# A decoder layer on one core: the down projection as seven block products

## The chip, the cores and the metric

The kernel runs on one core of a Trainium2 chip. The metric is the time of one execution on the device, in microseconds (us). TensorE does the matmuls, VectorE (DVE), ScalarE (ACT) and GpSimd (POOL) the rest, SyncE (SP) issues the transfers. Each engine takes its instructions in the order in which they were written for it. TensorE's order is written by hand; a scheduler lays out the others'.

## The reference

One layer for 1024 new tokens and 8 single ones (1032 columns in all), in fp32. This is the part around the change; `h` comes from two sequence mixers that share one input projection.

```python
h = rmsnorm(x, w['norm2_w'])
gate, val = jnp.split(h @ w['w_up'], 2, axis=-1)        # 1024 -> 2 x 2816
gate, buf_f_new = causal_dwconv(gate, buf_f, w['ffn_conv_w'], w['ffn_conv_b'])
x = x + (jax.nn.silu(gate) * val) @ w['w_down']         # 2816 -> 1024
...
y = rmsnorm(x, final_norm_w)
```

## The kernel before

The kernel is one stream of matmuls through four stages. Up to about 400 us run the input projections and the state-space mixer, from there to about 880 us the eight heads of the linear recurrence beside the rest of the input projections ("the heads"), then the output projection, from about 1056 to 1508 us the up projection, and from 1508 us the down projection with the final norm.

Data lies with features on partitions and tokens along the row. Every fp32 operand is split into a rounded part (ScalarE casts, `hi` or `wh`) and a remainder (VectorE subtracts, `lo` or `wl`), and each product is three matmuls: `wh*hi + wh*lo + wl*hi`. Weights come into `ws` (two buffers), tokens into `lo`, where they are split in place.

The up projection already uses seven products in place of eight block products (`ORDER`, class `Up`). It runs over 22 hidden tiles `j` of 128 features. For each, `up_load` fetches the weights of the next tile, GpSimd forms sums of them (`up_sums`), `up_split` splits them, 14 groups of 12 matmuls of 258 columns run (7 products x 2 token halves), and `up_close` does the convolution (ACT, then two taps on VectorE into `fcv`), SiLU, the product with `val`, and the store to `act_d`. The buffers of this stage (`fext`, `val`, `fcv`) come from one ring of five, `x5`.

The down projection contracts over the 22 hidden tiles in rounds of four (`RND`), five rounds, with the last two tiles apart. In a round each output tile `m` (8 of 128 features) meets four token quarters of 256, 256, 256 and 264; the partial sum in PSUM is added by VectorE to `xT[m]`, which holds the residual. The last two tiles run by token quarter, and after each quarter its token tiles are transposed by TensorE and go through the final norm (squares on ScalarE, root, scaling on VectorE, or ScalarE and GpSimd, store).

`tick()` stands after matmuls and runs work put there by `after(n, ...)`: it is written n ticks later. `spread(pieces, n)` writes one piece every n ticks. `fetch` puts a transfer behind the latest weight load on SP.

## Time and profile before

| | |
|---|---|
| median of 3 runs | 1781.38 us (1780.85 to 1782.73) |
| the profiled execution's own time | 1783.03 us |
| its span | 1781.3 us |
| mean granted TensorE clock | 0.994 |
| HBM read, written | 147.84 MB, 38.52 MB |

Rows of the profile read as follows. A group row gives line, engine, operation, out<-in, shapes, count, then busy time in us and mean ns of one, then the idle time just before on that engine and what ended it. A window row gives for each engine the busy us and the number of instructions, then the granted clock, the busy share of the transfer engines and GB/s. A wait row gives who waited for whom: us in total, times, longest. A timeline row gives start, duration, engine, line, and in brackets the idle time before. A tile row gives min, median and max ns, and the first and last start in us. `PE` is the matmul, `PEld` its weight load.

### The profile page before, as it was taken

Reading aid. Unit: us, or ns where it says so; the run is one execution under the profiler, and the core shown is the slowest. Engines: PE = TensorE matmul, PEld = TensorE weight load, DVE = VectorE, ACT = ScalarE, POOL = GpSimd, SP = SyncE. Lnnn points to the kernel's source line nnn. Section 1 sums busy time; section 2 is a strip of 40 time slices with the busy share of each in tenths; the row PEclk is TensorE's granted clock in tenths of the full one; section 3 lists DMA queues with packets and bytes.
Section 4 is the critical chain, followed back from the end, with each engine's and each line's share of the span. In section 5 each row is a group of like instructions: output and inputs, shape, how many; then the busy total and the mean of one; then the engine's idle time right before and its main releaser. Section 6 shows DMA issues by size and latency. Waiting matters only on the chain.

```text
span 1781.3 us, 38569 instructions
## 1 busy us (share of the span) xinstructions
PE 1740.1 (98%) x16223; PEld 1685.6 (95%) x16223; DVE 1118.6 (63%) x1949; ACT 797.7 (45%) x1413; POOL 394.5 (22%) x411
## 2 busy tenths in 40 slices
PE   7999999989999999999999999999999999999998
PEld 7999998989999999999999998999999999999997
DVE  4657888567655554556656678666666667545545
ACT  6477687444444444354344544334333344111114
POOL 1102142120110110111011234554445542000002
PEclk9999999999999999999999999999999999999999
DMA  5133575553222221224466432222222225422212
GB/s 155 36 88 84 150 209 151 141 168 106 66 78 63 76 82 43 82 79 127 145 193 200 125 114 72 72 72 78 81 92 72 72 82 204 152 82 90 97 60 96
DMA packets 240547, 188.66 MB, mean 106 GB/s; under 512 B 13356, under 2 KB 213590, under 8 KB 240358
## 3 DMA queue, kind: packets, MB, share of 16 engines
q1 hardware_dynamic: 240086, 186.11, 34.3%
q8 instruction: 127, 2.08, 0.5%
q14 instruction: 46, 0.38, 0.1%
q0 software_dynamic: 288, 0.10, 0.0%
HBM read 147.84 MB, written 38.52 MB: 105 GB/s over the span
## 4 chain that ended last, share of the span: by engine, by line
PE 72%; DVE 4%; DMA 2%; ACT 1%; issue 1%; DVEq 0%; POOL 0%; SPq 0%; ACTq 0%
PE mm L94 26%; PE ub L94 14%; PE dn L94 13%; PE ua L94 10%; PE a L94 3%; PE o L94 2%; PE kv L94 1%; DMA Sd<-in_state_ssm_dram 1%; DVE x L1260 1%; DMA ws<-in_w_out_dram 0%; PE ktp L960 0%; DVE wl L1056 0%; PE hms L94 0%; PE vtp L913 0%; DMA out_dram<-Sd 0%
## 5 line engine op out<-in xcount | busy, mean ns | idle before, releaser
L94 PE MATMUL mm<-hh,wh 128*128 128x344 f32 x1248 | 406.6, 326 | 0.0
L94 PE MATMUL mm<-hl,wh 128*128 128x344 f32 x1248 | 404.2, 324 | 0.0
L94 PE MATMUL mm<-hh,wl 128*128 128x344 f32 x1248 | 402.7, 323 | 0.0
L94 PEld LDWEIGHTS mm<-hh,wh 128*128 128x128 f32 x1248 | 234.9, 188 | 3.2 <-issue 1.1
L94 PEld LDWEIGHTS mm<-hl,wh 128*128 128x128 f32 x1248 | 234.9, 188 | 2.7 <-issue 1.1
L94 PEld LDWEIGHTS mm<-hh,wl 128*128 128x128 f32 x1248 | 235.0, 188 | 2.2 <-issue 1.0
L94 PE MATMUL ub<-uh,wh 128*128 128x258 f32 x704 | 199.5, 283 | 2.1 <-DVE fext L1431 1.6
L94 PE MATMUL ub<-ul,wh 128*128 128x258 f32 x704 | 199.9, 284 | 1.5 <-DVE ul L1292 1.5
L94 PE MATMUL ub<-uh,wl 128*128 128x258 f32 x704 | 199.0, 283 | 0.0
L94 PE MATMUL mm<-mx,wh 128*128 128x258 f32 x1024 | 191.3, 287 | 2.4 <-DVE mx L1072 2.0
L94 PE MATMUL dn<-ah,wh 128*128 128x256 f32 (+1 forms) x640 | 181.1, 283 | 1.0 <-DVE x L1556 0.9
L94 PE MATMUL dn<-ah,wl 128*128 128x256 f32 (+1 forms) x640 | 180.3, 282 | 0.0
L94 PE MATMUL dn<-al,wh 128*128 128x256 f32 (+1 forms) x640 | 180.3, 282 | 0.0
L189 ACT CAST wh<-ws 128x1024 fp32r<-128x1024 f32 x72 | 75.4, 1048 | 214.6 <-PE dn L94 136.0
L94 PEld LDWEIGHTS mm<-mx,wh 128*128 128x128 f32 x1024 | 159.2, 190 | 3.8 <-DVE mx L1072 2.4
L94 PE MATMUL ua<-uh,wh 128*128 128x258 f32 x528 | 150.1, 284 | 0.5 <-ACT us L1403 0.5
L94 PE MATMUL ua<-ul,wh 128*128 128x258 f32 x528 | 150.1, 284 | 0.0
L94 PE MATMUL ua<-uh,wl 128*128 128x258 f32 x528 | 149.9, 284 | 0.0
L94 PE MATMUL mm<-mx,wl 128*128 128x258 f32 x512 | 145.6, 284 | 1.5 <-DVE wl L1056 1.5
L94 PEld LDWEIGHTS ub<-uh,wh 128*128 128x128 f32 x704 | 133.0, 189 | 2.5 <-ACT uh L1270 1.8
L94 PEld LDWEIGHTS ub<-ul,wh 128*128 128x128 f32 x704 | 133.4, 189 | 1.9 <-DVE ul L1292 1.9
L94 PEld LDWEIGHTS ub<-uh,wl 128*128 128x128 f32 x704 | 133.4, 190 | 0.0
(339 smaller groups left out, 3747.6 us busy)
## 6 DMA issues: line engine op xcount, KB each, us to landing
ws<-in_w_in_dram SPq DMA_DIRECT2D x52, 512.0 KB
ws<-in_w_up_dram SPq DMA_DIRECT2D x44, 512.0 KB
ws<-in_w_out_dram SPq DMA_DIRECT2D x36, 512.0 KB
act_d<-val SPq DMA_DIRECT2D x22, 516.0 KB
al<-act_d SPq DMA_DIRECT2D x22, 516.0 KB
ws<-in_w_down_dram SPq DMA_DIRECT2D x22, 512.0 KB
mx<-mix_d SPq DMA_DIRECT2D x32, 258.0 KB
csb<-cs_d SPq DMA_DIRECT2D x32, 256.0 KB
```

What stands on the lines that cost most here:

```text
L94: PE.matmul(out, lhsT, rhs, start=start, stop=stop)
L189: A.copy(wh[:, :n], ws[:, :n])
L1260: V.scalar_tensor_tensor(x_, x_, col("n2", m), rs, op0=ALU.mult, op1=ALU.mult)
```

## The change

The down projection becomes seven block products over all 22 contraction tiles, one product after another. The 2816 features are paired, even tile with odd tile (11 pairs, `DK`); the 1024 outputs are cut into two halves of four tiles; the 1032 tokens into two halves of two spans (256 + 260 columns, `SPAN`). Each product takes a sum of token parts and a sum of weight parts (or a single part), and its result is added to or subtracted from several parts of `xT` (`PARTS`).

The token sums are formed in `up_close` (`act_sets`: two sums per even tile, six per odd) and stored to `act_d`, one plane per product. The weight sums are formed by GpSimd far earlier, while the heads run (`down_sums`, 22 pieces: two loads, four additions, one store to `wsum_d`), and are read back as weights of products p4 to p7.

A unit is one product for one output tile of the half: 66 matmuls (11 pairs x 3 x 2 token blocks). There are 28, the last product's being cut into single blocks at the end so that token tiles are finished in turn (`UNITS`). Weights are loaded two units ahead, split at tick 36 of the unit before; tokens are loaded and split during the product before. VectorE's splits are put behind the last eviction written (`pinned`). The final norm of a token tile runs after the unit that completes it (`FIN`); there is one more such tile, of four tokens. The ring `x5` becomes three rings, `xe`, `xc` and `xv` (six buffers). Half of the products' partial sums of the first five products now use four more PSUM tiles.

The diff, cut to its core:

```diff
-        "x5": (UW, 5), "us": (QW, 10), "t": (512, 4)}
+        "xe": (UW, 2), "xc": (UW, 1), "xv": (UW, 3), "us": (QW, 10), "t": (512, 4)}
...
+    wsum_d = dram.tile([2, 4, 2, P, DK, P], F32, name="wsum_d")
+    def down_sums():
+        src = w_down[0].rearrange("(i two p) (gv h c) -> h i p two gv c", two=2, p=P, gv=2, h=2)
+        for i in range(DK):
+            for h in range(2):
+                t = tl("g", "wq")[:, :DM]
+                for two in range(2):
+                    fetch(t[:, two * 512:(two + 1) * 512].rearrange("p (gv c) -> p gv c", gv=2), src[h, i][:, two])
+                yield
+                g1, v1, g2, v2 = (t[:, n * 256:(n + 1) * 256] for n in range(4))
+                for out, x_, y_ in ((v2, v1, v2), (v1, g1, v1), (g1, v2, g1), (g2, g1, g2)):
+                    G.tensor_tensor(out, x_, y_, op=ALU.add)
+                yield
+                SP.dma_start(wsum_d[h].rearrange("q m p k c -> p k (q m) c")[:, i],
+                             t.rearrange("p (q c) -> p q c", c=P))
+                yield
...
-    job("conv", None, once(lambda: spread(conv_states(), 60)))
+    job("conv", None, once(lambda: (spread(conv_states(), 60), spread(down_sums(), 26))))
...
-    act_d = dram.tile([FT, P, NT], F32, name="act_d")
+    act_d = dram.tile([7, DK, P, MID], F32, name="act_d")
+    PROD = ("p1", "p7", "p4", "p5", "p6", "p2", "p3")
+    SPAN = [[slice(0, 256), slice(256, 512)], [slice(512, 772), slice(772, NT)]]
+    BLOCK = [slice(0, 256), slice(256, MID)]
...
-        SP.dma_start(act_d[j], val[:, :NT])
+        spread(act_sets(j, ext, val), 6)
+    even = [None]
+    def act_store(name, i, t, c=None):
+        for n in range(2):
+            SP.dma_start(act_d[PROD.index(name), i, :, BLOCK[n]], t[:, BLOCK[n] if c is None else SPAN[n][c]])
+    def act_sets(j, ext, val):
+        i = j // 2
+        if j % 2 == 0:
+            even[0] = val
+            act_store("p1", i, val, 0)
+            yield
+            for n in range(2):
+                V.tensor_tensor(ext[:, BLOCK[n]], val[:, SPAN[n][0]], val[:, SPAN[n][1]], op=ALU.subtract)
+            act_store("p7", i, ext)
+            return
+        e = even[0]
+        act_store("p2", i, val, 0)
+        act_store("p4", i, val, 1)
+        yield
+        for n in range(2):
+            x_ = e[:, SPAN[n][1]]
+            V.tensor_tensor(x_, x_, val[:, SPAN[n][1]], op=ALU.subtract)
+        act_store("p5", i, e, 1)
+        yield
+        for n in range(2):
+            x_ = e[:, SPAN[n][0]]
+            V.tensor_tensor(x_, e[:, SPAN[n][1]], x_, op=ALU.subtract)
+        act_store("p6", i, e, 0)
+        yield
+        for n in range(2):
+            V.tensor_tensor(ext[:, BLOCK[n]], e[:, SPAN[n][0]], val[:, SPAN[n][0]], op=ALU.add)
+        act_store("p3", i, ext)
+    toks, wdn, evicted = {}, {}, [None]
+    def tok_open(n):
+        homes = ("hT",) * DK if n % 2 == 0 else ("hT",) * 5 + ("xe", "xe", "xc", "xv", "xv", "xv")
+        toks[n] = [tl(tag, "at", F32R) for tag in homes]
+    def tok_load(n, ks):
+        for k in ks:
+            SP.dma_start(toks[n][k][:, MID:NT].bitcast(F32), act_d[n, k])
+    def pinned(fn):
+        if evicted[0] is None:
+            return fn()
+        with tc.issue_after(evicted[0].ins):
+            fn()
+    def tok_split(n, ks):
+        for k in ks:
+            hi, lo = toks[n][k][:, :MID], toks[n][k][:, MID:NT]
+            A.copy(hi, lo.bitcast(F32))
+            pinned(lambda: V.tensor_tensor(lo, lo.bitcast(F32), hi.bitcast(F32), op=ALU.subtract))
+    SUMS = ("p6", "p5", "p4", "p7")
+    K1 = 8
+    def dw_load(u, n, m, pool):
+        name = PROD[n]
+        if name in SUMS:
+            src = wsum_d[m // 2, SUMS.index(name), m % 2]
+        else:
+            row, col_ = {"p1": (0, 0), "p2": (1, 0), "p3": (1, 512)}[name]
+            src = w_down[0].rearrange("(k two p) c -> two p k c", two=2, p=P)[row][:, :, col_ + m * P:col_ + (m + 1) * P]
+        ws = wpool.tile([P, KT * P], F32, tag="ws", bufs=2, name=nm("ws"))
+        w2 = pool.tile([P, KT * P], F32R, tag="wl", bufs=2, name=nm("w2"))[:, :(DK - K1) * P].bitcast(F32)
+        SP.dma_start(ws.rearrange("p (k m) -> p k m", m=P), src[:, :K1])
+        SP.dma_start(w2.rearrange("p (k m) -> p k m", m=P), src[:, K1:])
+        wdn[u] = pool, ws, w2
+    def dw_split(u):
+        pool, ws, w2 = wdn[u]
+        hi = pool.tile([P, KT * P], F32R, tag="wh", bufs=2, name=nm("wh"))
+        lo = pool.tile([P, KT * P], F32R, tag="wl", bufs=2, name=nm("wl"))
+        b = pool.tile([P, KT * P], F32R, tag="wh", bufs=2, name=nm("w2h"))
+        n = (DK - K1) * P
+        A.copy(hi, ws)
+        pinned(lambda: V.tensor_tensor(lo, ws, hi.bitcast(F32), op=ALU.subtract))
+        A.copy(b[:, :n], w2)
+        pinned(lambda: V.tensor_tensor(b[:, n:2 * n], w2, b[:, :n].bitcast(F32), op=ALU.subtract))
+        wdn[u] = [(hi, lo, k * P) if k < K1 else (b[:, :n], b[:, n:2 * n], (k - K1) * P) for k in range(DK)]
+    UNITS = [(n, m, (1, 0)) for n in range(6) for m in range(4)]
+    UNITS += [(6, 0, (1,)), (6, 1, (1,)), (6, 2, (1,)), (6, 3, (1, 0)), (6, 2, (0,)), (6, 1, (0,)), (6, 0, (0,))]
+    POOLS = [u % 2 for u in range(28)] + [None, 1, 0]
+    KEPT = {28: 26}
+    def unit_load(u):
+        if u < len(UNITS) and u not in KEPT:
+            dw_load(u, UNITS[u][0], UNITS[u][1], wpool if POOLS[u] else tmp)
+    def unit_split(u):
+        if u in KEPT:
+            wdn[u] = wdn[KEPT[u]]
+        elif u < len(UNITS):
+            dw_split(u)
+    def last_step(n):
+        if n == 3:
+            unit_load(0)
+            tok_open(0)
+        if n == 6:
+            tok_load(0, range(8))
+        if n == 9:
+            unit_split(0)
+            tok_load(0, range(8, 10))
+            tok_split(0, range(0, 4))
+        if n == 11:
+            tok_load(0, range(10, 11))
+            unit_load(1)
+            tok_split(0, range(4, 8))
+        if n == 12:
+            tok_split(0, range(8, 11))
...
+            if j == FT - 1:
+                last_step(n)
...
-        def down(w, kt, msl, acts, c):
-            q = quarters[c]
...
-                mm(ps, wh[:, msl], hi[:, q], start=(k == 0), stop=False)
-                mm(ps, wh[:, msl], lo[:, q], start=False, stop=False)
-                mm(ps, wl[:, msl], hi[:, q], start=False, stop=(k == kt - 1))
-            return ps
-        for r0 in range(0, FT - RND, RND):
...
-            for m in range(0, KT, 2):
-                wh, wl = wload(w_down[0, rows, m * P:(m + 2) * P], nk, 2 * P)
-                for i in range(2):
-                    for c, cs in enumerate(quarters):
-                        ps = down(lambda k: (wh[:, k, :], wl[:, k, :]), nk, slice(i * P, (i + 1) * P), acts, c)
-                        V.tensor_tensor(xT[m + i][:, cs], xT[m + i][:, cs], ps, op=ALU.add)
...
-    for c in (3, 0, 1, 2):
-        cs = quarters[c]
-        for m in range(KT):
-            ps = down(lambda k: wd[k], nk, slice(m * P, (m + 1) * P), acts, c)
-            V.tensor_tensor(xT[m][:, cs], xT[m][:, cs], ps, op=ALU.add)
-        for t0 in range(cs.start, cs.stop, P):
...
+        xT = [tl("big", "x1")[:, :NT] for _ in range(KT)]
+        for m in range(4):
+            for half_ in (0, 4):
+                SP.dma_start(xT[m + half_], x1_d[m + half_])
+        fw = tl("big", "fw")
+        SP.dma_start(fw[:, :DM], final_norm_w.unsqueeze(0).to_broadcast([P, DM]))
+        PARTS = {"p1": ((0, 0, 1), (0, 1, 1), (4, 1, 0), (4, 0, 0)), "p7": ((0, 1, 1), (4, 1, 0)), "p4": ((0, 1, 1),),
+                 "p5": ((4, 1, 1), (4, 0, 1)), "p6": ((0, 1, 1), (4, 1, 0), (4, 0, 0)), "p2": ((0, 0, 1),),
+                 "p3": ((4, 0, 1),)}
+        turn = [0]
+        def product(u, i):
+            n, m, _ = UNITS[u]
+            b = BLOCK[i]
+            turn[0] += 1
+            if n < 5 and turn[0] % 2:
+                ps = bank("dn")
+            else:
+                ps = psmm.tile([P, 512], F32, tag="mm", name=nm("dn"))
+            ps = ps[:, :b.stop - b.start]
+            for k in range(DK):
+                hi, lo = toks[n][k][:, b], toks[n][k][:, MID + b.start:MID + b.stop]
+                wh, wl, c0 = wdn[u][k]
+                wh, wl = wh[:, c0:c0 + P], wl[:, c0:c0 + P]
+                mm(ps, wh, hi, start=(k == 0), stop=False)
                 tick()
+                mm(ps, wh, lo, start=False, stop=False)
+                tick()
+                mm(ps, wl, hi, start=False, stop=(k == DK - 1))
+                tick()
+            for c0, c, plus in PARTS[PROD[n]]:
+                x_ = xT[m + c0][:, SPAN[i][c]]
+                evicted[0] = V.tensor_tensor(x_, x_, ps, op=ALU.add if plus else ALU.subtract)
+        def fin(t0, n, last):
...
-                if i and c != 2:
+                if i and not last:
...
+        FIN = {21: (256, P), 22: (384, P), 23: (772, P), 24: (900, 124), 25: (T, ND), 28: (512, P), 29: (640, P), 30: (768, 4)}
+        for u, (n, m, insts) in enumerate(UNITS):
+            after(2, lambda u=u: unit_load(u + 2))
+            after(36 if len(insts) > 1 else 6, lambda u=u: unit_split(u + 1))
+            if n < 6:
+                if m == 0:
+                    tok_open(n + 1)
+                if m < 3:
+                    ks = range(4 * m, min(4 * m + 4, DK))
+                    after(8, lambda n=n, ks=ks: tok_load(n + 1, ks))
+                if m:
+                    ks2 = range(4 * m - 4, min(4 * m, DK))
+                    pieces = (tok_split(n_, [k]) for n_ in [n + 1] for k in ks2)
+                    after(14, lambda pieces=pieces: spread(pieces, 12))
+            for i in insts:
+                product(u, i)
+            if u in FIN:
+                fin(*FIN[u], False)
+        for t0 in (0, P):
+            fin(t0, P, True)```

How it moves VectorE's order. First place: the end of the up projection and the first block of the down projection, before (`al`, `ah` are tokens, `wl` weight remainders, `x` the residual, `dn` the partial sum in PSUM):

```order
L1431 TENSOR_TENSOR fext_17732<-us_17843,ub_17892 128x258
L1431 TENSOR_TENSOR fext_17732<-us_17860,ub_17906 128x250
...
L190 TENSOR_TENSOR wl_18000<-ws_17998,wh_17999 128x1024
L1438 TENSOR_TENSOR val_17733<-us_17783,ua_17922 128x258
L356 SCALAR_TENSOR_TENSOR fcv_17950<-fext_17732,vcol,fcv_17950 128x1048
L1438 TENSOR_TENSOR val_17733<-us_17798,ua_17936 128x258
L356 SCALAR_TENSOR_TENSOR fcv_17950<-fext_17732,vcol,fcv_17950 128x1048
L1028 TENSOR_TENSOR al_17979<-al_17979,ah_17978 128x1032
L1556 TENSOR_TENSOR x_2353_18004<-x_2353_18004,dn_18006 128x256
L1454 TENSOR_TENSOR val_17733<-val_17733,fext_17732 128x1032
```

The same place on VectorE now (`at` are token tiles, L1501 to L1510 the sums of tokens, L1695 the evictions, `wl_18494` and `w2h_18495` the weights of unit 1):

```order
L1453 TENSOR_TENSOR fext_18110<-us_18240,ub_18314 128x258
L1533 TENSOR_TENSOR at_18195<-at_18195 128x516
L1533 TENSOR_TENSOR at_18196<-at_18196 128x516
L1453 TENSOR_TENSOR fext_18110<-us_18265,ub_18328 128x250
...
L1476 TENSOR_TENSOR val_18111<-val_18111,fext_18110 128x1032
L1695 TENSOR_TENSOR x_2374_18402<-x_2374_18402,dn_18431 128x260
L1501 TENSOR_TENSOR val_17842<-val_17842,val_18111 128x256
...
L1510 TENSOR_TENSOR fext_18110<-val_17842,val_18111 128x260
L1695 TENSOR_TENSOR x_2374_18402<-x_2374_18402,dn_18431 128x260
L1695 TENSOR_TENSOR x_2378_18406<-x_2378_18406,dn_18431 128x260 x2
L1558 TENSOR_TENSOR wl_18494<-ws_18345,wh_18493 128x1024
L1560 TENSOR_TENSOR w2h_18495<-w_2370_18346,w2h_18495 128x384
```

The splits of the last two token tiles of the first product now stand ahead of the last gate eviction, and the six sums and the block's evictions stand ahead of unit 1's weights.

Second place: SP in one of the heads, before (`ws` weights of the input projection, `Sh` a head's states, `vd` and `vb` its values on their way through memory):

```order
L179 DMA Sh_7196<-in_state_hgrn_dram 128x4x128
L179 DMA Sh_7200<-in_state_hgrn_dram 128x4x128
L977 DMA out_dram<-SS_7009 128x128
L186 DMA ws_7426<-in_w_in_dram 128x8x128
L855 DMA vd_d<-vd_7192 8x128
```

and now:

```order
L179 DMA wq_7469<-in_w_down_dram 128x2x256 x2
L179 DMA Sh_7288<-in_state_hgrn_dram 128x4x128
L179 DMA Sh_7292<-in_state_hgrn_dram 128x4x128
L1166 DMA wsum_d<-wq_7469 128x8x128
L977 DMA out_dram<-SS_7090 128x128
L186 DMA ws_7526<-in_w_in_dram 128x8x128
L179 DMA wq_7716<-in_w_down_dram 128x2x256 x2
L1166 DMA wsum_d<-wq_7716 128x8x128
L855 DMA vd_d<-vd_7284 8x128
```

Loads of down weights and the stores of their sums stand between the head's own transfers; each store waits for GpSimd's four additions.

41 lines of the change are left out of this document (6 added, 35 removed).

## The prediction

> **What bounds the kernel now.** I read the page's first part, then the table of windows over the last stages, then the waits of TensorE and the tiles of the stage that the change rewrites.
>
> ```profile
> span 1781.3 us, 38569 instructions
> PE 1740.1 (98%) x16223; PEld 1685.6 (95%) x16223; DVE 1118.6 (63%) x1949; ACT 797.7 (45%) x1413; POOL 394.5 (22%) x411
> ```
> ```profile
> core 0: us, PE busy (x) PEld busy (x) DVE busy (x) ACT busy (x) POOL busy (x), PEclk, DMA share, GB/s
> 300.00:400.00 100.00, 94.03 (x610) 90.19 (x609) 58.76 (x99) 45.16 (x98) 18.40 (x15) 0.97 0.58 166
> 700.00:800.00 100.00, 100.00 (x1430) 95.31 (x1428) 57.75 (x98) 44.58 (x67) 16.52 (x12) 1.00 0.25 74
> 1400.00:1500.00 100.00, 100.00 (x835) 100.00 (x834) 65.14 (x108) 38.79 (x69) 42.22 (x47) 1.00 0.31 99
> ...
> 1508.40:1741.20 232.80, 231.84 (x1943) 230.98 (x1943) 117.80 (x209) 41.67 (x42) 0.00 (x0) 1.00 0.29 98
> 1741.20:1771.70 30.50, 30.01 (x253) 29.15 (x252) 19.49 (x53) 16.66 (x43) 8.94 (x7) 1.00 0.26 96
> ```
>
> TensorE is busy for 98% of the span, and a busy bar alone proves little where matmuls overlap, so I take the spacing. In 1400 to 1500, 835 matmuls, nearly all 258 columns wide, take 100 us: 0.1198 us each. The down projection's five rounds hold 1943 in 232.80 us, again 0.1198. Two different stages with one spacing, the weight loads beside it as full, and a granted clock of 1.00: the stage is paced by the number of matmuls, not by what feeds them. The waits say the same.
>
> ```profile
> PE ub L94 <- DVE fext L1431: 1.6, 1, 1.6
> ...
> PE dn L94 <- DVE x L1556: 0.9, 1, 0.9
> ```
>
> In the down projection TensorE waited once, 0.9 us. VectorE, at 117.80 of 232.80 us, has half the stage free.
>
> **What goes.** The down projection has 22 contraction tiles x 8 output tiles x 4 token quarters x 3 products of halves = 2112 matmuls, of 256, 256, 256 and 264 columns, 258 on average. The block form has 7 products x 11 contraction tiles x 4 output tiles x 2 token blocks x 3 = 1848, of 256 and 260, again 258. So 264 x 0.1198 = **31.6 us** go from TensorE, if all that feeds it stays hidden.
>
> **What is added beside it.** The durations:
>
> ```profile
> L1556 DVE TENSOR_TENSOR x<-x,dn 128x256 f32<-128x256 f32 x120 | 49.8, 418 | 67.9 <-PE dn L94 67.9
> L190 DVE TENSOR_TENSOR wl<-ws,wh 128x1024 fp32r<-128x1024 f32 x20 | 24.5, 1223 | 8.1 <-ACT wh L189 8.0
> L189 ACT CAST wh<-ws 128x1024 fp32r<-128x1024 f32 x19 | 20.0, 1050 | 136.0 <-PE dn L94 136.0
> L1593 DVE SCALAR_TENSOR_TENSOR ot<-fin,fss,fw 128x512 f32<-128x512 f32 x10 | 7.3, 748 | 0.4
> ...
> L1381 DVE TENSOR_TENSOR wl<-ws,wh 128x512 fp32r<-128x512 f32 x63 | 43.4, 689 | 0.8
> L1522 DVE COPY cfr<-l 10x512 f32<-10x512 f32 x5 | 3.4, 677 | 0.1
> ```
>
> From 512 to 1024 elements VectorE's subtraction grows by 0.534 us, so I take 0.69 for 516, 0.55 for 384 and 0.41 for 256.
>
> The up projection (22 hidden tiles of 168 matmuls, 20.1 us each) gains 8 subtractions or additions per pair of tiles, 8 x 0.41 = 3.3 us in 40 us where VectorE has 35% free. They stand between two evictions of PSUM tiles that TensorE wants back four groups later. Price: nothing. SP's stores there rise from 2 to 14 per pair. They wait for these sums, and the next weight load waits behind them, but its first half is split only about 4 us after it lands, and is used in the next tile.
>
> The down stage: TensorE would need 1848 x 0.1198 = 221 us. VectorE has 112 evictions x 0.42 = 47, 77 token splits x 0.69 = 53, 30 weight splits x (1.22 + 0.55) = 53, and 20 us for the copies and the final norm: 173 us. It fits on average. In the first product it doesn't: 32 evictions (13.4), 4 weight splits (7.1), 11 token splits (7.6), the last hidden tile's convolution, product and six sums (7.1) and the first copy are 36 us in 31.6. So VectorE's order there has to be walked.
>
> **The entry into the first product.** Before, at the same place:
>
> ```profile
> 1507.25 1.26 ACT L354 ACTIVATE fcv<-fext,vcol 128x1048 f32<-128x1048 f32 x1 [0.54 <-DVE last L1435]
> 1511.54 1.06 ACT L1452 ACTIVATE fext<-fcv 128x1024 f32<-128x1024 f32 x1 [1.13 <-DVE fcv L356]
> ...
> 1508.60 1.30 DVE L356 SCALAR_TENSOR_TENSOR fcv<-fext,vcol,fcv 128x1048 f32<-128x1048 f32 x1
> 1512.85 1.22 DVE L1454 TENSOR_TENSOR val<-val,fext 128x1032 f32<-128x1032 f32 x1
> ```
> ```profile
> 1489.79 0.34 SPq L1511 DMA_DIRECT2D al<-act_d  x1
> ...
> 1493.32 1.06 ACT L1027 CAST ah<-al 128x1032 fp32r<-128x1032 f32 x1 [1.10 <-DMA al<-act_d]
> ```
>
> Let E be the end of the up projection (1508.4 before). TensorE starts the first block at once: its tokens come from even hidden tiles. But token tile 10 takes a buffer that TensorE frees at E-2.9 (two groups of twelve matmuls before E). Half the bytes of the load above (3.5 us from issue to use) I put at 2.5 to 3 us, so its cast ends near E+0.6 and its split at E+1.2. In VectorE's order that split stands ahead of the last gate eviction, which was ready at E-2.9. Then: evictions to E+2.2; ScalarE's start of the convolution, behind the weight cast of unit 1 (its load is issued at E-2.3), E+2.1 to 3.3; VectorE's two taps and an eviction to E+6.3; SiLU to 7.6; product to 8.8; one eviction, six sums, three evictions to 12.9; then unit 1's weight split, E+14.1. TensorE needs it at E+7.9 (66 matmuls): **6.2 us** lost. Were the loads early, the same walk gives E+9.7, 1.8 us. By the same steps units 2 and 3 arrive in time, and unit 4's split, behind four more token splits and a copy, is 1.7 us late. I take 7.9 us; bounds 2 and 12 (the latter if loads take 2 us more and both later units are also late). From the second product on a unit needs at most 7 of its 7.9 us on VectorE, and the debt is paid back.
>
> The short units at the end (4.0 us each) need 1.5 us of ScalarE and 1.8 of VectorE for weights and, by the tail's rows below, 2.6 and 1.1 for a tile of the final norm: together 4.1 and 2.9, just enough. Nothing; bound +5.
>
> **Transfers.** The stage moves 30 weight sets x 0.72 MB (128 x 1408 x 4 bytes), 77 token tiles x 0.264 and some 11 MB of residual, outputs and last stores, 53 MB in 221 us, 240 GB/s. The row 300 to 400 moved 166 GB/s at 0.58 busy, so 286 at full. They are issued a unit or more ahead. Nothing; the bound is a rival.
>
> **The heads.** 22 loads of down weights, 88 GpSimd additions and 22 stores run beside the head stage.
>
> ```profile
> L1416 POOL TENSOR_TENSOR val<-us,us x41: 735/757/1734, 1100.7 to 1502.9; 128x258 f32<-128x258 f32 x41
> L886 DVE TENSOR_TENSOR k<-k,tt x43: 680/693/1683, 421.9 to 860.0; 128x512 f32<-128x512 f32 x43
> ...
> DVE k L886 <- PE a L94: 57.3, 40, 2.8
> PE a L94 <- DVE q L887: 1.0, 1, 1.0
> ...
> 597.98 1.28 POOL L869 TENSOR_TENSOR Sh<-Sh,vb 128x512 f32<-128x512 f32 x1
> L94 PE MATMUL od<-Sh,qb x16: 272/273/297, 621.0 to 621.4; 128*32 128x128 f32 x16
> ```
>
> 88 x 0.75 = 66 us of GpSimd, which is 17% busy there. Each store holds SP until load and sums are done, about 6 us (a load of some 3 us, as above, and four sums of 0.75). What is queued behind it, the small transfer of v to memory and the head's state update, ends at 599.3 before and is used at 621.0: 22 us of cover. VectorE waits 1.4 us per level (57.3 / 40) for TensorE, so delays below that vanish. I take 0.6 us; bounds 0 and 35 (below).
>
> **The tail.** From the last matmul to the span's end there are 9.6 us. Now a four-token tile stands ahead of the last two tiles of the final norm.
>
> ```profile
> L1583 ACT ACTIVATE ot<-fin 128x512 f32<-128x512 f32 x16 | 9.4, 595 | 30.2 <-PE fin L1581 28.6 <-PE dn L94 0.9 <-DMA out_dram<-ot 0.3
> L1590 ACT ACTIVATE ot<-fin,fss 128x512 f32<-128x512 f32 x6 | 4.1, 687 | 1.3 <-DVE fss L1586 1.3
> L1583 ACT ACTIVATION_READ_ACCUMULATOR ot<-fin 128x1 f32 x16 | 3.2, 198 | 0.0
> L1585 ACT ACTIVATE fss<-fss,epsc 128x1 f32<-128x1 f32 x8 | 2.4, 296 | 2.3 <-DVE fss L1584 2.3
> ...
> 1771.40 0.28 PE L94 MATMUL dn<-ah,wdl 128*128 128x256 f32 x1
> ...
> 1776.56 1.41 DVE L1593 SCALAR_TENSOR_TENSOR ot<-fin,fss,fw 128x512 f32<-128x512 f32 x2
> ```
>
> It puts 2 x 0.79 us of squares, a root and a scaling on ScalarE, and 0.75 on VectorE, ahead of them, and takes two of the four PSUM tiles. Walking the steps the last output is ready 8.4 us after the last matmul, where it was 6.3: **+2.1 us**, bounds 0.5 and 3.
>
> **Sum.** -31.6 + 7.9 + 0.6 + 2.1 = -21.0 us. The profiled run's span is 1781.3, its own time 1783.03 and the median 1781.38; a saving inside the span shifts all three, so 1781.38 - 21.0 = **1760.4 us**.
>
> **Rivals.** (1) All is hidden: 1781.4 - 31.6 + 2.1 and 2 at the entry = 1754. For it: half-idle VectorE; against: the walk above. 0.22.
>
> (2) VectorE and ScalarE stay late. If each of the first three products lost what the first does, the stage would lose 7.9 x 3: 1776. For it: every weight split stands behind an eviction of the same unit, so debt moves on to TensorE; against: the later units' surplus. 0.10.
>
> (3) Slower: GpSimd's sums block the heads. L886 takes 0.69 us, and up to 1.68, one GpSimd instruction more. A run of four sums is 3 us; if all 22 runs met a level of the scan chain and each cost 3.0 - 1.4 us, 35 us, then 1760.4 + 35 = 1795. It turns the sign where a run costs over 0.95 us. Against it: TensorE waited once on this chain, 1.0 us, although GpSimd ran 3 us runs there already. 0.04. The Trainium skill (SBUF — State Buffer, Who interferes with whom) says that a VectorE instruction with two SBUF inputs and a GpSimd instruction that reads SBUF share a port pair held for a whole instruction. By that rule up to 66 us of VectorE's time would go, still within its free 40% of about 370 us, and the sum would stand; the 1.68 us row agrees with the rule.
>
> (4) Transfers bind. At 200 GB/s the 53 MB would take 265 us, 44 more than TensorE needs: 1760.4 + 44 = 1804. Against it: the 286 above. 0.02.
>
> **How the numbers follow.** The forecast has 0.62. Eight times in ten the time lies from 1751 (rival 1 with the tail hidden) to 1776 (rival 2). A measurement of this kernel can tell about 0.2%, 3.6 us. Faster than 1777.8: the forecast, rival 1 and most of rival 2, 0.92; within: 0.03; slower: rivals 3 and 4, 0.05.
>
> **What would show it.** Matmuls 264 fewer at an unchanged 0.12 us; between E and E+40 one or two waits of TensorE on VectorE's weight split, 6 and 2 us; none on DMA later; no new wait in the heads; the tail 11 to 12 us. It is wrong if the spacing in the later products grows, or if the heads take over 3 us more.

## The result, and the profile after

The changed kernel takes 1759.99 us (median of 4 runs, 1758.13 to 1761.37) against 1781.12 for the kernel before; the ratio is 0.9884, 95% interval 0.9872 to 0.9896. The forecast was 1760.4. The total came out right; the terms of the sum did not, and this section says where.

The first lines of the page and TensorE's waits behind the up projection, in the changed kernel (waits: who for whom, us in total, times, longest):

```profile
span 1756.2 us, 39052 instructions
...
PE 1710.0 (97%) x15967; PEld 1655.9 (94%) x15967; DVE 1173.3 (67%) x2053; ACT 844.8 (48%) x1512; POOL 482.8 (27%) x500
```
```profile
PE dn L94 <- DVE wl L1558: 3.9, 1, 3.9
PE fin L1702 <- DVE ot L1714: 1.8, 1, 1.8
```

256 matmuls fewer (264 in the down projection, 8 transposes of the final norm more), and two new waits: one on VectorE's split of weights, the one the forecast walked to, and one in the tail. This span is 25.1 us shorter than that of the first profile of before, while the medians differ by 21.1. One pair of profiles is too little for terms of a few us, so I cut every trace of this study into the same stages. A stage runs from the first start of one kind of matmul to the first or last start of another, as the tile rows give them: the heads from the first `a` to the last `o`, the output projection from there to the first `ua`, the up projection to the first `dn`, the down projection to the last `dn`, the tail to the end of the span. For the heads these are the two rows of the changed kernel, 883.6 - 401.4 = 482.2 us:

```profile
L94 PE MATMUL a<-q,k x3456: 176/196/270, 401.4 to 868.2; 128*32 128x32 f32 x160, 128*16 128x16 f32 x32
...
L94 PE MATMUL o<-q,SS x112: 275/275/275, 442.6 to 883.6; 128*128 128x128 f32 x112
```

| trace | to the heads | heads | output proj. | up | down | tail |
|---|---|---|---|---|---|---|
| before, first trace | 401.3 | 481.6 | 173.2 | 452.4 | 262.9 | 9.9 |
| before, second (rep_before) | 402.7 | 479.5 | 172.8 | 452.4 | 263.3 | 9.8 |
| changed, first | 401.4 | 482.2 | 173.6 | 452.4 | 233.9 | 12.7 |
| changed, second (rep_after) | 398.4 | 483.9 | 174.2 | 451.2 | 235.4 | 12.7 |
| fin4_early | 404.5 | 484.4 | 173.4 | 451.7 | 236.6 | 9.8 |
| split1_only | 402.5 | 487.4 | 175.3 | 452.4 | 235.6 | 12.7 |
| split1_load2 | 405.5 | 484.4 | 173.8 | 451.2 | 236.5 | 12.7 |
| entry_nofin | 402.4 | 485.4 | 173.0 | 451.2 | 234.2 | 12.7 |
| entry_split12 | 403.7 | 485.3 | 173.8 | 452.3 | 228.8 | 12.7 |
| best_safe | 400.5 | 486.4 | 173.6 | 451.7 | 230.4 | 9.8 |
| no_sum_adds | 401.9 | 478.3 | 174.2 | 451.1 | 235.1 | 13.2 |
| no_sum_all | 399.6 | 479.4 | 173.7 | 450.5 | 235.3 | 13.1 |
| sum_memset | 400.7 | 479.4 | 174.1 | 450.6 | 233.6 | 12.7 |
| sums_up | 402.5 | 479.8 | 173.3 | 537.4 | 235.1 | 12.7 |

Eight traces (from changed, first, to best_safe) have the heads, the output projection and the up projection unaltered. Their means against the two of before: to the heads +0.4, heads +4.4 (484.9 against 480.55), output projection +0.8, up -0.6; down -28.45 and tail +2.85 from the two traces of the changed kernel. The sum is -20.6, in agreement with the medians. The first trace of the changed kernel is that of the fastest of its four executions (1758.13 us) and has the shortest heads of the eight; the first trace of before is that of an execution at 1783.03, above the median. The two differ by 24.9 us, and that made the 25.

The wait at the entry, in the changed kernel. First VectorE's timeline (start, duration, engine, line; E, the end of the up projection, is 1509.6), then windows of 2 to 4 us with TensorE's matmuls and its granted clock (third column from the right):

```profile
1515.99 1.23 DVE L1476 TENSOR_TENSOR val<-val,fext 128x1032 f32<-128x1032 f32 x1 [1.29 <-ACT fext L1475]
1517.14 0.42 DVE L1695 TENSOR_TENSOR x<-x,dn 128x260 f32<-128x260 f32 x1
1517.48 0.76 DVE L1501 TENSOR_TENSOR val<-val,val 128x256 f32<-128x256 f32 x2
1518.15 0.76 DVE L1506 TENSOR_TENSOR val<-val 128x256 f32<-128x256 f32 x2
1518.83 0.76 DVE L1510 TENSOR_TENSOR fext<-val,val 128x256 f32<-128x256 f32 x2
1519.50 1.09 DVE L1695 TENSOR_TENSOR x<-x,dn 128x260 f32<-128x260 f32 x3
1520.51 1.22 DVE L1558 TENSOR_TENSOR wl<-ws,wh 128x1024 fp32r<-128x1024 f32 x1
```
```profile
1517.50:1521.50 4.00, 0.36 (x3) 0.15 (x2) 4.00 (x11) 0.00 (x0) 0.00 (x0) 1.00 0.68 179
1521.50:1523.50 2.00, 1.72 (x8) 1.73 (x9) 2.00 (x6) 0.00 (x0) 0.00 (x0) 0.59 1.06 374
1523.50:1525.50 2.00, 2.00 (x12) 2.00 (x12) 0.01 (x1) 0.00 (x0) 0.00 (x0) 0.56 0.88 231
1525.50:1527.50 2.00, 2.00 (x19) 2.00 (x19) 0.17 (x1) 0.26 (x1) 0.00 (x0) 1.00 1.10 333
```

Product, six sums and evictions, then unit 1's weights: the order of the forecast's walk. The split of `wl`, the remainder that TensorE waits for, ends at 1521.73, E+12.1 (E+13.0 in the second trace), where the walk said E+14.1. The windows show what the walk did not have: after the gap the granted clock is 0.56 to 0.59, and TensorE starts 12 matmuls in 2 us where it starts 19 afterwards. It stays so for about 3.6 us, some 16 matmuls at 0.216 us in place of 0.118: another 1.6 us.

The tail, TensorE's and ScalarE's timelines in the changed kernel:

```profile
1747.37 1.10 PE L1702 MATMUL fin<-ident,x 128*128 128x128 f32 x8 [1.80 <-DVE ot L1714]
...
1748.81 0.60 ACT L1704 ACTIVATE ot<-fin 128x512 f32<-128x512 f32 x1 [1.10 <-DMA out_dram<-ot]
...
1750.36 0.60 ACT L1704 ACTIVATE ot<-fin 128x512 f32<-128x512 f32 x1 [0.86 <-DMA out_dram<-ot]
```

The last token tile waits for a PSUM tile, as forecast, and then twice for the store of an earlier output, since the `ot` tiles come from a ring of four buffers and the extra tile of four tokens takes two of them.

### The profile page after: what moved, and what is told of

Its sections match the earlier page's. It is cut to its first block, busy times and chain, and to the rows that moved or that the text cites. A ratio compares the mean times of both kernels' runs of the same rounds, so it can differ in the third digit from the quotient of the medians.

```text
span 1756.2 us, 39052 instructions
## 1 busy us (share of the span) xinstructions
PE 1710.0 (97%) x15967; PEld 1655.9 (94%) x15967; DVE 1173.3 (67%) x2053; ACT 844.8 (48%) x1512; POOL 482.8 (27%) x500
## 4 chain that ended last, share of the span: by engine, by line
PE 70%; DVE 5%; issue 1%; ACT 1%; DMA 1%; POOLq 0%; DVEq 0%; POOL 0%; ACTq 0%
PE mm L94 25%; PE ub L94 14%; PE dn L94 12%; PE ua L94 11%; PE a L94 2%; PE o L94 2%; PE kv L94 1%; DVE k L886 1%; DVE x L1282 1%; DVE q L887 1%; DMA ws<-in_w_out_dram 1%; DVE wl L1056 1%; PE ktp L960 0%; PE hms L94 0%; PE vtp L913 0%
## 5 line engine op out<-in xcount | busy, mean ns | idle before, releaser
L94 PE MATMUL mm<-hh,wh 128*128 128x344 f32 x1248 | 407.1, 326 | 0.0
L94 PE MATMUL mm<-hl,wh 128*128 128x344 f32 x1248 | 404.6, 324 | 0.0
L94 PE MATMUL mm<-hh,wl 128*128 128x344 f32 x1248 | 403.2, 323 | 0.0
L94 PEld LDWEIGHTS mm<-hh,wh 128*128 128x128 f32 x1248 | 235.4, 189 | 3.2 <-issue 1.1
L94 PEld LDWEIGHTS mm<-hl,wh 128*128 128x128 f32 x1248 | 235.4, 189 | 2.7 <-issue 1.1
L94 PEld LDWEIGHTS mm<-hh,wl 128*128 128x128 f32 x1248 | 235.3, 189 | 2.2 <-issue 1.0
L94 PE MATMUL ub<-uh,wh 128*128 128x258 f32 x704 | 199.5, 283 | 2.1 <-DVE fext L1453 1.6
L94 PE MATMUL ub<-ul,wh 128*128 128x258 f32 x704 | 199.9, 284 | 1.5 <-DVE ul L1314 1.5
L94 PE MATMUL ub<-uh,wl 128*128 128x258 f32 x704 | 199.0, 283 | 0.0
L94 PE MATMUL mm<-mx,wh 128*128 128x258 f32 x1024 | 191.0, 286 | 1.6 <-DVE mx L1072 1.2
L94 PE MATMUL dn<-at,wh 128*128 128x260 f32 (+1 forms) x896 | 164.3, 284 | 0.0
L94 PEld LDWEIGHTS mm<-mx,wh 128*128 128x128 f32 x1024 | 158.5, 189 | 3.3 <-DVE mx L1072 1.7
L94 PE MATMUL ua<-uh,wh 128*128 128x258 f32 x528 | 150.2, 284 | 0.5 <-ACT us L1425 0.5
L94 PE MATMUL ua<-ul,wh 128*128 128x258 f32 x528 | 150.2, 284 | 0.0
L94 PE MATMUL ua<-uh,wl 128*128 128x258 f32 x528 | 149.9, 284 | 0.0
L94 PE MATMUL mm<-mx,wl 128*128 128x258 f32 x512 | 145.4, 284 | 1.7 <-DVE wl L1056 1.7
L94 PEld LDWEIGHTS dn<-at,wh 128*128 128x128 f32 x896 | 138.9, 190 | 0.0
L94 PEld LDWEIGHTS ub<-uh,wh 128*128 128x128 f32 x704 | 133.0, 189 | 2.5 <-ACT uh L1292 1.8
L94 PEld LDWEIGHTS ub<-ul,wh 128*128 128x128 f32 x704 | 133.4, 189 | 1.9 <-DVE ul L1314 1.9
L1164 POOL TENSOR_TENSOR wq<-wq 128x256 f32<-128x256 f32 x88 | 82.1, 933 | 189.6 <-DMA wq<-in_w_down_dram 184.4
L94 PEld LDWEIGHTS ub<-uh,wl 128*128 128x128 f32 x704 | 133.4, 190 | 0.0
L94 PE MATMUL dn<-at,wl 128*128 128x260 f32 (+1 forms) x448 | 127.4, 284 | 3.9 <-DVE wl L1558 3.9
```

What stands on the lines that cost most here:

```text
L94: PE.matmul(out, lhsT, rhs, start=start, stop=stop)
L1164: G.tensor_tensor(out, x_, y_, op=ALU.add)
```

## Experiments: the terms repeated

The changed kernel and the kernel before, unaltered, for second traces.

> The changed kernel once more, nothing altered. The first pair of profiles differs by 25 us in span, the medians by 21 us, and my sum of terms gave 21. Theory A: the terms are those of the first trace (entry wait 3.9 us plus 1.6 us at a lower clock, heads +0.7, tail +2.9), the trace was a fast one by chance, and the scatter of 3 us between executions lies ahead of the up projection: the second trace shows the same 3.9, 0.7 and 2.9 within 0.5 us, time 1758 to 1761. Theory B: the scatter lies in the entry, where the weights come through a busy transfer queue: the wait differs by over 1 us between the two traces.

Measured: 1759.93 us (0.9887, 0.9867 to 0.9907). The entry wait was 4.9 us instead of 3.9, the heads 483.9 instead of 482.2, the stretch ahead of them 398.4 instead of 401.4; the tail was the same. Neither theory holds alone: the entry scatters by 1 us, and the heads by 1.7 and the part ahead of them by 3.

> The kernel before once more, nothing altered, for a second trace: the heads (first a matmul to last o matmul) took 481.5 us in the first trace of before and 482.2, 483.9, 484.4, 487.4 and 484.4 in five traces of changed kernels. Theory A (the down weights' sums in the heads cost more than the forecast's 0.6 us, 2 to 5 us): before's second trace gives 481 to 482.5. Theory B (the heads scatter by themselves): it gives 483 or more.

Measured: 479.5 us of heads, below the 481 to 482.5 of theory A and further still from theory B's 483. Before is at or below its first trace, and all eight traces with the sums lie above both, which is theory A's point; but the two traces of before are 2.1 us apart, so the heads scatter too.

## Experiments: the sums in the heads

In no_sum_adds the four additions per piece are taken out, as below; in no_sum_all the whole `spread(down_sums(), 26)`, and the products p4 to p7 read parts of the down weights in place of their sums:

```diff
-                for out, x_, y_ in ((v2, v1, v2), (v1, g1, v1), (g1, v2, g1), (g2, g1, g2)):
-                    G.tensor_tensor(out, x_, y_, op=ALU.add)
```

> The changed kernel with GpSimd's 88 additions of down weights left out; the 44 loads and the 22 stores stay, so what is stored is the loaded parts and not their sums. Theory A (GpSimd's instructions hold VectorE and the head's state update): the heads go back to 481.5 to 482.5 us and the time falls by 2 to 3 us. Theory B (the transfers: SyncE's queue, and TensorE's instructions that come through the same transfer engines, its waits of 1.6 to 3.1 us with no releaser): the heads stay at 483 to 485 us, time within 1 us of 1760.

> The changed kernel with the loads, additions and stores of the heads all left out; products p4 to p7 read parts of the down weights in place of their sums, the same number of bytes. Both theories of no_sum_adds: the heads go back to 481.5 to 482.5 us and the waits of TensorE without a releaser vanish there; the time falls by 2 to 3 us, to 1757 to 1758. If the heads stay at 484 us, neither the additions nor the transfers are the cause.

Measured: 1755.12 us (0.9857, 0.9836 to 0.9878) and 1754.97 (0.9857, 0.9837 to 0.9877), heads 478.3 and 479.4. That is 5 us less than the changed kernel, twice the 2 to 3 us of theory A, and the same within the scatter with and without the 44 loads and 22 stores. So the additions cost it, and the transfers nothing that shows.

What is it about the additions? sum_memset keeps GpSimd busy as long, without reading:

```diff
-                for out, x_, y_ in ((v2, v1, v2), (v1, g1, v1), (g1, v2, g1), (g2, g1, g2)):
-                    G.tensor_tensor(out, x_, y_, op=ALU.add)
+                for c in (0, 256, 0, 256):
+                    G.memset(t[:, c:c + 768], 1.0)
```

> The 88 additions of down weights replaced by 88 GpSimd memsets of 768 columns, 0.73 us each by the traced 0.98 us for 1032: GpSimd is held as long, but reads nothing from SBUF; the stored parts are constants. In the changed kernel VectorE's busy time between 430 and 800 us is 219 to 224 us against 206 in before and in no_sum_adds, and L886's mean rises from 0.76 to 0.87 us. Theory A (VectorE and GpSimd share a port to SBUF, and each VectorE instruction that meets an addition takes longer): with memsets VectorE's busy time there returns to 206 to 209 us, the heads to 478 to 481 us, and the time is 1755 as in no_sum_adds. Theory B (GpSimd's own queue: the head's state update and the small transfers wait behind four instructions in a row): the heads stay at 483 to 485 us and the time at 1760.

Measured: 1755.47 us (0.9859, 0.9843 to 0.9876), heads 479.4. Below, for the second trace of before, the second of the changed kernel, and sum_memset, each time first the window 430 to 800 (PE, PEld, DVE, ACT and POOL busy us, clock, DMA share, GB/s), then groups within it: a step of the scan chain, and GpSimd's work on the down weights (count, busy us, mean ns).

```profile
430.00:800.00 370.00, 369.48 (x4811) 351.89 (x4810) 206.79 (x372) 160.15 (x246) 49.79 (x36) 1.00 0.25 73
```
```profile
L886 DVE TENSOR_TENSOR k<-k,tt 128x512 f32<-128x512 f32 x35 | 27.5, 786 | 46.1 <-PE a L94 46.1
```
```profile
430.00:800.00 370.00, 365.15 (x4760) 347.68 (x4759) 220.78 (x370) 158.99 (x243) 130.33 (x124) 1.00 0.45 132
```
```profile
L886 DVE TENSOR_TENSOR k<-k,tt 128x512 f32<-128x512 f32 x34 | 31.0, 912 | 44.7 <-PE a L94 44.7
...
L1164 POOL TENSOR_TENSOR wq<-wq 128x256 f32<-128x256 f32 x88 | 80.8, 918 | 191.2 <-DMA wq<-in_w_down_dram 154.7 <-DVE qb L856 31.3
```
```profile
430.00:800.00 370.00, 369.35 (x4827) 351.51 (x4826) 208.07 (x372) 160.50 (x247) 114.83 (x124) 1.00 0.45 133
```
```profile
L886 DVE TENSOR_TENSOR k<-k,tt 128x512 f32<-128x512 f32 x35 | 27.7, 791 | 46.4 <-PE a L94 46.4
...
L1164 POOL MEMSET wq<- 128x768 f32 x88 | 65.5, 745 | 201.7 <-DMA wq<-in_w_down_dram 167.3 <-DVE qb L856 30.6
```

GpSimd is busy for 65 us more than before in sum_memset, and VectorE only 1.3 us more; with additions VectorE has as many instructions as before (370 against 372), 14 us more to do, and the step of the chain takes 912 ns instead of 786. TensorE is busy 365.15 us of the window instead of 369.4. Its waits in this window, first in the second trace of before (sum_memset has the same one row), then in the second of the changed kernel:

```profile
PE cst L342 <- DVE od L671: 0.5, 1, 0.5
```
```profile
PE a L94 <- issue: 2.3, 2, 1.3
PE a L94 <- DVE q L887: 2.1, 4, 0.8
...
```

About half of the loss is TensorE waiting for a step of the chain (L887 is the step behind L886). The other half are waits for which the profile shows no releaser (`issue`). All eight traces with the additions in the heads have such waits before `a` matmuls, 1.3 to 3.1 us in the heads, and the other six have none: the additions bring them, but in what way stays open.

So it is not GpSimd's queue (theory B falls) but the reading: each engine's instructions stretch where they meet, GpSimd's too (918 ns against the 750 of the forecast). The Trainium skill (SBUF — State Buffer, Who interferes with whom) states just this: a VectorE instruction with two SBUF inputs contends with a GpSimd instruction that reads SBUF, and not with one that only writes it. These runs agree, with 14 us against 1.3.

Part of the scatter of the heads is TensorE's granted clock. In the first trace of before, split1_only, entry_nofin, entry_split12 and best_safe it is 0.50 for one stretch of 3.4 us in the heads (two of the five are shown in the last section), in the other nine it is not. Without these five the heads take 483.7 us with the additions (four traces) and 479.3 without (five): 4.4 us again.

Then the sums were moved, with nothing left out, from the heads into the up projection:

```diff
-    job("conv", None, once(lambda: (spread(conv_states(), 60), spread(down_sums(), 26))))
+    job("conv", None, once(lambda: spread(conv_states(), 60)))
...
                 up_load(j + 1)
+            if n == 3 and j == 2:
+                spread(down_sums(), 40)
```

> The sums of down weights are formed during the up projection (from its third hidden tile, a step every 40 ticks), no more in the heads; nothing left out. Theory A (what they cost is VectorE's delay in the heads' chain of short steps, and the up projection has room for it): heads back at 478 to 481 us, the up stage stays within 1 us of 451 to 452.4, time about 1755.5. Theory B (VectorE's delay turns up wherever GpSimd adds): the up stage grows by 3 us or more and the time stays within 1.5 us of 1760.

Measured: 1842.19 us (1.0333, 1.0316 to 1.0350). The heads went back to 479.8, as theory A said, and the up stage grew by 85 us, far beyond the 3 us or more of theory B. TensorE's granted clock was 0.94 in that stage. Its waits between 1080 and 1560:

```profile
ACT wh L1402 <- POOL wt L1379: 109.0, 37, 9.7
...
PE ub L94 <- ACT us L1433: 54.2, 14, 8.9
POOL wq L1164 <- DMA wq<-in_w_down_dram: 43.1, 6, 8.9
```

In the up projection GpSimd forms the sums of the next tile's weights (L1379). The down sums stand ahead of them in its queue and wait for their own loads; ScalarE's cast waits for GpSimd 37 times, and behind that cast stand ScalarE's evictions, for which TensorE waits, 54.2 us. So here it is a queue. An output projection with the sums in it was not run.

## Experiments: the entry into the first product

split1_only writes unit 1's split ahead of the last tile's convolution (and no more at tick 36 of unit 0); split1_load2 also loads unit 2 early. The core of both:

```diff
+        if j == FT - 1:
+            unit_split(1)
         up_close(j, us_[0])
...
             tok_split(0, range(4, 8))
+            unit_load(2)
```

> VectorE's and ScalarE's split of unit 1's weights is written ahead of the convolution of the last hidden tile, no more behind its sums; the loads stay where they are. Theory A (the forecast's walk: VectorE's order alone is what TensorE waits for): the wait of 3.9 us and the 1.6 us at a low clock behind it go, and nothing comes in their place: 5.5 us less, about 1754.5. Theory B (SyncE's queue is next): unit 2's weights are issued only behind the stores of the last hidden tile, near E+11, and landed at 1527.2 in the first trace; TensorE without its first wait asks for them at E+15.8 = 1525.4 and now waits there for 4 to 6 us, with the low clock behind it: within 1.5 us of 1760.

> As split1_only, and unit 2's load is written ahead of the end of the up projection, so it is issued ahead of the residual's loads and of those stores. Theory A (VectorE's order alone): the same as split1_only, 1754.5. Theory B (SyncE's queue is next): this one, and not split1_only, is 5 to 6 us faster than the changed kernel, about 1754.5, with no wait of TensorE over 0.5 us between E and E+40 and a granted clock of 1.00 there.

Measured: 1761.79 us (0.9896, 0.9877 to 0.9916) and 1764.2 (0.9905, 0.9888 to 0.9923). In split1_only the wait came as theory B said, with the median 0.3 us outside its 1.5; split1_load2 did not gain what theory B said, so neither theory holds for the pair. Rows of the timelines of TensorE, ScalarE and SP's queue, first split1_only (E is 1517.5), then split1_load2 (E is 1514.9):

```profile
1537.66 0.80 PE L94 MATMUL dn<-at,wh 128*128 128x260 f32 x2 [4.27 <-ACT wh L1557]
...
1536.56 1.04 ACT L1557 CAST wh<-ws 128x1024 fp32r<-128x1024 f32 x1 [10.38 <-DMA ws<-in_w_down_dram]
...
1527.48 1.79 SPq L1483 DMA_DIRECT2D act_d<-val  x4
...
1529.84 0.40 SPq L1547 DMA_DIRECT2D ws<-in_w_down_dram  x1
```
```profile
1544.18 0.80 PE L94 MATMUL dn<-at,wh 128*128 128x260 f32 x2 [4.62 <-ACT wh L1557]
...
1543.08 1.04 ACT L1557 CAST wh<-ws 128x1024 fp32r<-128x1024 f32 x1 [3.21 <-DMA ws<-in_w_down_dram]
...
1535.41 0.89 SPq L1483 DMA_DIRECT2D act_d<-fext  x2
1536.34 0.50 SPq L1547 DMA_DIRECT2D ws<-in_w_down_dram  x1
```

In split1_only TensorE passes unit 1 without a wait and waits 4.3 us for unit 2. Those weights were issued only behind the stores of the last tile's product, which hold SP until that product is there, and then took 6.7 us to land (1529.84 to 1536.56) among 2.07 MB of loads and stores that moved between 1529 and 1537. In split1_load2 unit 2 passes with 0.7 us, and TensorE waits 4.6 us for unit 3, whose load stands behind the stores of the six sums and again takes 6.7 us. The wait moved on by a unit each time it was taken away.

entry_nofin keeps both edits, puts the sums and stores of the last tile 30 ticks apart instead of 6, loads the residual's tiles one unit before each is needed, and the norm's weights at unit 10. The core of it:

```diff
-        spread(act_sets(j, ext, val), 6)
+        spread(act_sets(j, ext, val), 6 if j < FT - 1 else 30)
...
+            if u < 3:
+                after(4, lambda u=u: x_load(u + 1))
+            if u == 10:
+                after(4, fw_load)
```

> Four moves at the entry, none at the tail: unit 1's split ahead of the convolution and unit 2's load early, as in split1_load2; the last hidden tile's sums and stores 30 ticks apart and not 6; the residual's pairs 1 to 3 loaded one unit before each is needed, and the norm's weights at unit 10, so that some 3 MB leave the queue of transfers between E-8 and E+20. Theory A (SyncE's queue and the backlog of transfers behind it make each later unit's weights late, so that a wait taken away comes back one unit on): no wait of TensorE over 1 us between E and E+45, no low clock, stage 5 to 6 us shorter than in the second trace of the changed kernel, time about 1754.5. Theory B (VectorE and ScalarE have too much work in the first product, wherever it is put): a wait of 3 us or more comes back at unit 3 or 4, and the time stays within 2 us of 1760.

Measured: 1760.61 us (0.9887, 0.9872 to 0.9901). Instead of one wait there are three, all on VectorE; below them a piece of VectorE's timeline:

```profile
1529.55 0.39 PE L94 MATMUL dn<-at,wl 128*128 128x260 f32 x1 [1.52 <-DVE wl L1558]
1540.85 0.39 PE L94 MATMUL dn<-at,wl 128*128 128x260 f32 x1 [2.76 <-DVE wl L1558]
1550.42 0.39 PE L94 MATMUL dn<-at,wl 128*128 128x260 f32 x1 [1.03 <-DVE wl L1558]
...
1537.02 1.30 DVE L1533 TENSOR_TENSOR at<-at 128x516 fp32r<-128x516 f32 x2 [4.51 <-ACT at L1532]
1538.23 1.43 DVE L1707 TENSOR_TENSOR x<-x,dn 128x260 f32<-128x260 f32 x4
1539.58 1.22 DVE L1558 TENSOR_TENSOR wl<-ws,wh 128x1024 fp32r<-128x1024 f32 x1
```

Neither theory as put: no wait is over 3 us, but all three are over 1, and the median has not fallen. At 1537 VectorE has stood idle for 4.5 us on a token tile that is needed only in the next product, with evictions and the wanted weight split behind it. The stage is 1.2 us shorter than in the changed kernel's second trace (0.3 longer than in its first) although the waits add up to more, since the clock stays at 1.00 there. entry_split12 writes the split at the start of the unit before, ahead of all that:

```diff
-            after(36 if len(insts) > 1 else 6, lambda u=u: unit_split(u + 1))
+            after(12 if len(insts) > 1 else 6, lambda u=u: unit_split(u + 1))
```

> As entry_nofin, and each unit's weight split is written at tick 12 of the unit before and not at tick 36, so that it stands ahead of that unit's evictions and token splits. entry_nofin had three waits on VectorE's weight split left, 1.5, 2.8 and 1.0 us, with the loads landed in time for two of them. Theory A (the order on VectorE is what is left): the three waits go, the down stage takes 229 to 230 us (234.2 in entry_nofin), time about 1755. Theory B (late token loads, on which VectorE's in-order queue stands still with the weight split behind them): at least one wait of over 2 us is left and the stage stays above 232.5 us.

Measured: 1755.59 us (0.9856, 0.9842 to 0.9871), the down stage 228.8 us. All of TensorE's waits in it and the tail (the first row is the tail's):

```profile
PE fin L1714 <- DVE fss L1717: 1.8, 1, 1.8
PE l L1654 <- DVE cfr L1656: 0.3, 1, 0.3
```

Theory A. The changed kernel's stage was 233.9 and 235.4, so the entry cost it 5.1 to 6.6 us, its wait and the low clock behind it.

## Experiments: the tail, and a faster version

fin4_early runs the final norm of the tile of four tokens after unit 27, three units earlier:

```diff
-        FIN = {21: (256, P), 22: (384, P), 23: (772, P), 24: (900, 124), 25: (T, ND), 28: (512, P), 29: (640, P), 30: (768, 4)}
+        FIN = {21: (256, P), 22: (384, P), 23: (772, P), 24: (900, 124), 25: (T, ND), 27: (768, 4), 28: (512, P), 29: (640, P)}
```

> The final norm of the four tokens 768 to 771 is run after unit 27, three units earlier; nothing else. Theory A: the 2.9 us by which the tail is longer (12.5 us from the last down matmul to the end, 9.6 before) are this tile alone: the tail comes back to 9.6 to 10.2 us, and the time falls by 2.4 to 2.9 us. Theory B: the tail is longer because the last unit is one of the short ones, with its weights and an eviction close to the end: the tail stays above 11.5 us and the time falls by less than 1 us.

Measured: 1760.63 us (0.9882, 0.9862 to 0.9901). The tail is 9.8 us, as theory A said, but the time did not fall by its 2.4 to 2.9 us. In the trace the down stage is 236.6 us, 1.2 more than in the changed kernel's second, as the tile's transposes now stand in it and the entry wait was 5.4 us in that execution. Down stage and tail together are 246.4 us, against 246.6 and 248.1 in the changed kernel's two traces: 0.2 to 1.7 us, and single runs scatter by more.

best_safe is entry_split12 and fin4_early together:

> entry_split12 and fin4_early together, nothing left out. Theory A (the two losses are apart): the down stage as in entry_split12 plus about 1 us for the sixteen transposes that move into it, 229.5 to 230.5 us, with no wait of TensorE over 0.5 us there, the tail 9.5 to 10.2 us, the heads 482 to 487 us as in all kernels with the additions; time 1753 to 1754, 6 to 7 us below the changed kernel. Theory B (the tail's gain is eaten, as fin4_early's median, equal to the changed kernel's, may suggest): time 1755 to 1756.5, the same as entry_split12.

Measured: 1754.28 us (0.9848, 0.9833 to 0.9863), down 230.4, tail 9.8, heads 486.4. By the stages theory A holds, but for one wait of 0.7 us for a token split where it allowed 0.5: 230.4 + 9.8 is 1.3 us less than entry_split12's 228.8 + 12.7. The median lies between the two theories. It is the lowest median here of a kernel that leaves nothing out, 27.2 us below before in its own comparison, where the changed kernel was 20 to 21 below; that it beats entry_split12 (26.7 below) is within the scatter.

## Why the prediction was right, and where it was not

**Fewer matmuls: -31.6; measured -34.3.** The direction and the size hold. Without its entry wait the stage takes 228.8 us (entry_split12), 34.3 less than the 263.1 of before. Waits of 0.9 and 0.4 us that before had, against 0.3 in entry_split12, account for 1.0 of the other 2.7; where the rest sat, no view showed.

**The entry: +7.9; measured 5.1 to 6.6.** The place, the engine and the order of work were as walked. The split came 1 to 2 us sooner: in the first trace the token splits were done by E+0.4 and not E+1.2, and the convolution started earlier with them; in the second they were done by E+1.3, as walked, and the steps behind them were shorter by 1 us in all. The second term, 1.7 us at unit 4, never came: TensorE was already 5.5 us late there, which covers 1.7; lateness of two units on one path should not have been added. The 1.6 us of low clock was not in the sum at all. And "units 2 and 3 arrive in time" was right only because unit 1 made TensorE late; split1_only and split1_load2 showed both waiting behind it. The walk took VectorE's queue and left out SP's.

**The heads: +0.6; measured +4.4** (5.3 against all six traces without the additions there). This is the step that failed: "VectorE waits 1.4 us per level (57.3 / 40) for TensorE, so delays below that vanish." 57.3 us over 40 waits is a mean; it does not say that each level has 1.4 us to give. Between 430 and 800 us TensorE waited four times for a step of the chain, where it had not waited once. VectorE's 14 us more between 430 and 800 came with over 4 us of TensorE, though VectorE was busy for only 60% of that time. Rival 3 named the right mechanism, a VectorE instruction that lasts a GpSimd instruction longer, and priced it at its worst case of 35 us; an eighth of that is what came, about half of it as such waits and half without a visible releaser. That by the port rule "the sum would stand" was wrong for the same reason: a free share of an engine was taken for cover.

**The tail: +2.1; measured +2.85.** The walk through ScalarE, VectorE and PSUM was right. The two waits on stores, from a ring of four output buffers, were left out of it.

**The sum** held by luck: heads and tail together were 4.6 us too cheap, and entry and matmuls 4.8 us too dear, with the entry at the middle of its two values. Rival 2 did not occur: no wait is left after the first product. Rival 4 did not occur as put, but "nothing" for the transfers was too bold: at the entry they were late for units 2 and 3 once TensorE was not. Of what was to show it, the matmuls, the absence of later waits on DMA and the tail (12.7 for 11 to 12) came nearly as said; of the two waits at the entry one came; new waits did come in the heads, which took over 3 us more, and that the forecast had named as a sign of being wrong.

## What to carry to other kernels

A total that fits proves no term: cut both traces into stages, take a second trace of each kernel, and hold each term against its stage. Where a chain of short steps passes between two engines, a mean idle share is no cover, and filler work on GpSimd that reads SBUF can delay it even where GpSimd has time; nothing urgent may stand behind the filler in its queue either. When a wait is to be removed, walk every in-order queue at that place, the one that issues transfers too, or the wait comes back one unit later.

## What the hardware showed that was not expected

In the down projection TensorE's clock fell after single gaps of 3.6, 3.9 and 4.9 us, and not after 2.8. The windows behind them: first sum_memset (gap 3.6), then the changed kernel's second trace (4.9), then entry_nofin, with the end of its longest gap (2.8) inside:

```profile
1518.00:1520.00 2.00, 2.00 (x12) 2.00 (x11) 0.43 (x2) 0.00 (x0) 0.00 (x0) 0.50 0.97 254
```
```profile
1520.00:1522.00 2.00, 1.21 (x5) 1.21 (x6) 2.00 (x5) 0.00 (x0) 0.00 (x0) 0.50 0.98 360
```
```profile
1540.00:1545.00 5.00, 4.15 (x34) 4.15 (x35) 4.54 (x10) 1.90 (x4) 0.00 (x0) 1.00 1.00 366
```

The gap of 3.9 us so cost 5.5, and entry_nofin's three shorter ones only themselves. The Trainium skill (TensorE: Matmul & The Clock Gate, What's actually happening) has the clock halved after an idle window of about 3.4 us and restored after as long a busy one. These gaps agree with the first; the clock came back 3.6 us after the gap in the changed kernel's first trace and 4.6 us after it in the second.

But the length of a gap is not all that counts. In the heads of the same entry_nofin the clock fell after a gap of 1.65 us among small matmuls (first block: the gap, the 3.4 us with it, and the 3.4 us behind), and in those of the first trace of before after two waits of 0.9 and 1.1 us (second block):

```profile
801.68 0.29 PE L94 MATMUL a<-q,k 128*16 128x16 f32 x16 [1.65 <-issue]
...
799.00:802.40 3.40, 1.75 (x71) 1.40 (x70) 0.36 (x1) 0.46 (x1) 0.00 (x0) 0.99 0.39 105
802.40:805.80 3.40, 3.40 (x14) 3.40 (x13) 1.29 (x3) 1.61 (x4) 0.00 (x0) 0.50 0.02 5
```
```profile
838.00:841.00 3.00, 3.00 (x74) 2.60 (x73) 2.46 (x4) 1.17 (x2) 0.00 (x0) 0.50 0.30 113
```

What decides there was not tested. So in these traces a short gap is not safe by its length alone.
